# Four pairs of k tiles in w_up's second units, some weight sums made by adding DMAs, and two changes of order

## The chip, the core and the metric

The kernel runs on one core of a Trainium2 chip. The metric is the device time of one execution in microseconds (us); less is better. The core's engines work through instruction lists of their own and wait for each other by semaphores: TensorE (PE) multiplies and transposes, VectorE (DVE) and ScalarE (ACT) do elementwise work, GpSimd (POOL) and SyncE (SP) here mostly issue DMAs. A PE matmul takes its operands from SBUF and adds into a PSUM bank.

## The reference, cut to what matters

```python
u = rms_norm(x, norm_mix_w)                    # x: 256 x 2048, fp32
hq, hf, hi, hg, aq, ak, av, gates = split(u @ w_in)
y_a = rms_norm(hgrn2_scan(silu(hq), 1 - g, hi, log(g))) * silu(hg)
y_b = chunk_band_attention(aq, ak, av, rel_bias)
gate_a, gate_b = split(sigmoid(gates))
merged = gate_a * (y_a @ w_branch_a) + gate_b * (y_b @ w_branch_b)
h = x + merged @ w_out
u = rms_norm(h, norm_mlp_w)
h = h + square(relu(u @ w_up)) @ w_down        # w_up 2048 x 8192
out = rms_norm(h, norm_final_w)
```

Nearly all the time is in products of 256 rows with large fp32 weight matrices.

## The kernel before, in words

**One product.** An fp32 product is made of three matmuls (`mm3`, L145): each operand is split into a rounded high part and a low rest, and high by high, high by low and low by high are added. Weights come in raw tiles of 128 x 1024 (two k tiles by 512 columns, or one k tile by two column blocks; 512 KB) by a DMA on SP (`piece`, L673, issues at L681 and L684), and `parts` (L688) makes the high part `wh` by an ACT cast (L92) and the low part `wl` by a DVE subtraction (L93). There are eight raw buffers and six each for `wh` and `wl`; a load waits until its buffer's last reader is done, and a cast until PE is done with its buffer.

**One unit.** `gemm_s` (L720) makes 256 rows by two column blocks of 512 (n0, n1) over 16 k tiles. Of these k tiles, r pairs (k, k+4) are done together by the Strassen-Winograd scheme: seven products in place of eight. Products p1 to p7 go in the order p1, p3, p5, p2, p6, p7, p4. Their weight operands are sums of raw tiles, made in place by DVE (`adds`, L769, whose operation is L745): W22 += W12, W12 += W11, W11 += W22, W21 += W11. Their activation operands S4, S5, S2 and S7 are sums of blocks, made once per activation by `combos` (L615). What is not paired goes as plain tiles, named r0_k and r1_k for the first and second column block. With r = 4 pairs a unit has no half tiles; with r = 3 it has two tiles X and Y whose halves belong to different pairs, and their sums are of 512 columns. The names in the profile follow: `wl_dn10p` is the low part of a Strassen operand in the unit dn10, `wh_up12r` a high part of a plain tile in up12, `raw_dn` a raw tile.

**The MLP.** It runs in four quarters (qd 0 to 3) of 2048 hidden columns. A quarter has two units of w_up (up{qd}0 and up{qd}2, L1048) and two of w_down (dn{qd}0 and dn{qd}2, L1099), so that dn10 follows up12. The results of w_up are scaled, clipped and squared by ACT (`done`, L1042 and L1043), and transposed by PE into the activation u (`turn`, L1012; `tp_u`), which ACT and DVE split again; `turns` (L1028) transposes what waits, and when the first two of the four blocks of u are there, `combos` makes u's S sums for both units of w_down. The last plain tile of a unit is kept back and done within the next unit (`late`, `flush`). Results of w_down are copied by ACT and added to h by a DMA of POOL (`out_of`, L1074).

**The opening and the branches.** The kernel opens with the transposed projections hf and hq, for which PE takes pairs of k tiles as they arrive; `mm_t` (L172) makes for each k tile a matmul of 256 columns with the low weights and one of 512 with the high ones, for each of two column blocks. After the gates' projection come w_branch_a and w_branch_b: units ba0 and bb0 by `gemm_s` with r = 2 over 8 k tiles, then ba2, bb2, ba3, bb3 by `gemm2` (L705), which makes 512 columns at a time. `turn` transposes the merged blocks m0 to m3, `combos` makes their sums, and w_out's units wo0 (r = 3) and wo2 (r = 2) follow.

**What sets the order.** The functions write the instructions in one sequence; a list scheduler with priorities then orders each engine's list. Splits, weight sums and evictions carry a high priority (`tc.high_priority`). An engine executes its list strictly in order.

Of the kernel before, what the change touches and what calls it, by code (L numbers as in the profile page):

```python
# [12 lines left out]
ALU = mybir.AluOpType  # L13
# [3 lines left out]
P = 128  # L17
T = 256
NM = T // P
D = 2048  # L20
KD = D // P
# [29 lines left out]
def tile_hybrid_block(  # L51
# [120 lines left out]
    def mm_t(acc, rhs, nkt, kt, wh, wl):  # L172
        r = rhs[kt // 4][:, kt % 4]
        for cb in range(2):
            c = slice(cb * P, (cb + 1) * P)
            if kt:
                nc.tensor.matmul(acc[:, cb, 0:T], wl[:, c], r[:, 0, :], start=False, stop=False)  # L177
            nc.tensor.matmul(acc[:, cb, :], wh[:, c], r.rearrange("p u t -> p (u t)"),  # L178
                             start=kt == 0, stop=kt == nkt - 1)
            if kt == 0:  # L180
                nc.tensor.matmul(acc[:, cb, 0:T], wl[:, c], r[:, 0, :], start=False, stop=False)

    def add_parts(dst, acc):
        with tc.high_priority(offset=2000):
            nc.scalar.copy(dst, acc[:, :, T:])
            nc.vector.tensor_tensor(dst, acc[:, :, 0:T], dst, op=ALU.add)  # L186
# [17 lines left out]
        nc.sync.dma_start(xr, x[m * P:(m + 1) * P, :])  # L204
        nc.scalar.activation(xr, xr, AF.Square, accum_out=xsq[:, m:m + 1])

    done = [0, 0]
    for kt, n in zip(starts, steps):
        c, a = kt // 4, kt % 4
        xw = h2(f"xw{kt}")[:, :n]  # L210
        nc.sync.dma_start(xw, x_t[:, kt:kt + n, :])
        with tc.high_priority(offset=2000):
            for j in range(n):
                g, hi = wmix[:, kt + j:kt + j + 1], xT[c][:, a + j, 0, :]
                if kt < 2:
                    nc.vector.tensor_scalar(hi, xw[:, j, :], g, None, op0=ALU.mult)
                else:
                    nc.scalar.activation(hi, xw[:, j, :], AF.Copy, scale=g)
                nc.vector.scalar_tensor_tensor(xT[c][:, a + j, 1, :], xw[:, j, :], g, hi.bitcast(F32),
                                               op0=ALU.mult, op1=ALU.subtract)  # L220
        for i in range(2):
            while done[i] < kt + n:
                mm_t(accs[i], xT, KD, *next(ws[i]))
                done[i] += 1
    def rows(factors, what):

        wide = hp.tile([P, NM, P], F32, name=f"wide_{what}", tag="wide", bufs=1)
# [489 lines left out]
        with tc.high_priority(offset=2000):  # L717
            nc.vector.tensor_tensor(dst, acc, dst, op=ALU.add)

    def gemm_s(lhs, S, w, n0, what, done, r=R, kt0=0, between=None, front=None, fresh=False, tail=False, nkt=KD, room=None):  # L720

# [45 lines left out]
        def adds(As, Bs):  # L769
            for a, b in zip(As, Bs):  # L770
                add(a[0], b[0])
# [72 lines left out]
        if r == 3:  # L844
            mm("21", comb(7), px, (1, 2))
        u2 = copy(space(f"u2_{what}"), "21")
        adds(W21, W11)
        short = tail or len(left) == 2
        early = left[1][1] // 4 < len(lhs) and not short
        if early:  # L850
# [64 lines left out]
    def turn(n):  # L915
        mT.append(new_act(f"m{n}"))
        hi, lo = mT[n][:, :, 0, :], mT[n][:, :, 1, :]
        for m in range(NM):
            tp = transpose4(ga[n][m], f"m{n}{m}")
            split(hi[:, :, m * P:(m + 1) * P], lo[:, :, m * P:(m + 1) * P], tp)  # L920
# [27 lines left out]

    gemm_s(ya, Sy[0], w_branch_a, 0, "ba0", done_a, r=2, nkt=8, room=more[0])
    gemm_s(yb, Sy[1], w_branch_b, 0, "bb0", done_b, r=2, nkt=8, room=more[1])  # L950
    for n in range(2, 4):
        for y, w, gate, what in ((ya, w_branch_a, ga[n], "ba"), (yb, w_branch_b, gb[n], "bb")):
            acc = gemm2(y, w, n * NC, 8, f"{what}{n}", {2: flush, 6: lambda: turn(0)} if what == "ba" and n == 2 else {})
            for m in range(NM):
                gated(gate, m, acc[m])
            if (what, n) in (("bb", 2), ("ba", 3)):
                turn(len(mT))
                if n == 2:
                    Sm = combos(mT, "m", "b")
        for m in range(NM):  # L960
            both(n, m)

# [44 lines left out]
    for qd in range(NQ):  # L1007
        last = qd == NQ - 1
        uT = []
        pend = []  # L1010

        def turn(ahead=0):  # L1012

            c, rs = pend.pop(0)
            uT.append(new_act(f"u{qd}{c}"))
            hi, lo = uT[-1][:, :, 0, :], uT[-1][:, :, 1, :]
            for m in range(NM):
                tp = transpose4(rs[m], f"u{qd}{c}{m}")
                if c < 2:
                    blocks[m, c] = tk.tile([P, 4, P], F32, name=f"a{m}{c}_u{qd}", tag="t", bufs=TOK)  # L1020
                    nc.scalar.copy(blocks[m, c], tp)
                with tc.high_priority(offset=ahead):
                    split(hi[:, :, m * P:(m + 1) * P], lo[:, :, m * P:(m + 1) * P], tp)

        Su = {}
        blocks = {}

        def turns():  # L1028
            if len(hT) == 2:
                h_blocks(2)  # L1030
            while pend:
                turn()
            if len(uT) == 2:
                Su.update(combos(uT, f"u{qd}", "b", [blocks[m, j] for m in range(NM) for j in range(2)], 4))

        for c in range(0, 4, 2):
            rs = {}

            def done(m, n, acc, c=c, rs=rs):
                t = token(f"r{qd}{c}")  # L1040
                with tc.high_priority(offset=2000):
                    nc.scalar.activation(t, acc, AF.Relu, scale=rstd2[:, m:m + 1])  # L1042
                nc.scalar.activation(t, t, AF.Square)  # L1043
                rs[m, n] = t
                if m == NM - 1:
                    pend.append((c + n, [rs[i, n] for i in range(NM)]))

            gemm_s(hT, Sh, w_up, qd * (FF // NQ) + c * NC, f"up{qd}{c}", done, r=R if c else 4 if qd else 2, between=turns)  # L1048
            if not qd and not c:
                for i, s in combos(hT, "h4", None, ks=slice(R, 4), into=[Sh4[:, i:i + 1] for i in range(4)]).items():  # L1050
                    Sh[i] += s

        if last:
            wf = apool.tile([P, D], F32, name="wf", tag="act")
            nc.gpsimd.dma_start(wf, bass.AP(tensor=norm_final_w.tensor, offset=norm_final_w.offset, ap=[[0, P], [1, D]]))

        def weigh(m, n):

            t = h1[n][m]
            total = ssq3[:, m, n:n + 1] if n < 3 else rest3[:, m:m + 1]  # L1060
            nc.scalar.activation(token(f"ysq_{n}_{m}"), t, AF.Square, scale=D ** -0.5, accum_out=total)
            if n == 3:
                h1[n][m] = token(f"yw_{m}")
            nc.vector.tensor_tensor(h1[n][m], t, wf[:, n * NC:(n + 1) * NC], op=ALU.mult)

        def out_of(m, n, acc, last=last):
            r = h1[n][m]
            if last and n > 1:
                evict(r, acc)
            else:  # L1070
                t = token(f"y{qd}{n}{m}")
                with tc.high_priority(offset=2000):
                    nc.scalar.copy(t, acc)  # L1073
                nc.gpsimd.dma_start(r, t, accum_op=ALU.add)  # L1074
            if not last or n < 2:
                return
            if n == 2 and not m:
                for i in range(2):
                    for j in range(NM):
                        weigh(j, i)  # L1080
            weigh(m, n)
            if n < 3:
                if m:
                    nc.vector.tensor_reduce(most3, ssq3, axis=AX.X, op=ALU.add)
                return
            f = rstd3[:, m:m + 1]
            nc.vector.tensor_tensor(rest3[:, m:m + 1], rest3[:, m:m + 1], most3[:, m:m + 1], op=ALU.add)
            nc.gpsimd.tensor_tensor(f, rest3[:, m:m + 1], mhalf[:, 0:1], op=ALU.pow)
            for i, a, b, eng in ((0, 0, NC, nc.scalar), (2, 0, NC, nc.vector), (3, 0, NC, nc.vector),
                                 (1, 0, T, nc.scalar), (1, T, NC, nc.vector)):  # L1090
                t = h1[i][m][:, a:b]
                if eng is nc.scalar:
                    nc.scalar.activation(t, t, AF.Copy, scale=f)
                else:
                    nc.vector.tensor_scalar(t, t, f, None, op0=ALU.mult)
                (nc.scalar if eng is nc.scalar else nc.sync).dma_start(out[m * P:(m + 1) * P, i * NC + a:i * NC + b], t)

        for n0 in (0, 2):
            gemm_s(uT, Su, w_down, n0 * NC, f"dn{qd}{n0}", lambda m, n, acc, n0=n0: out_of(m, n0 + n, acc), r=4, kt0=qd * KD,  # L1099
                   front=None if n0 else lambda: turn(2000), between=None if n0 else turns, tail=last and n0 == 2)  # L1100


# [42 lines left out]
```

## Time and profile before

| what | value |
|---|---|
| median of 3 runs | 1401.89 us (1401.4 to 1402.52) |
| the profiled execution, its own time | 1402.0 us |
| span of that execution in the trace | 1400.0 us |
| mean granted TensorE clock | 0.998 |
| adding of weight sums by DVE in w_down (64) and w_up (44 full ones) | 77.3 and 53.4 us |
| loads over the span | 280 MB, 200 GB/s |

A line of the waits reads: engine and instruction that waited, the one it waited for, microseconds in total, times, longest. A line of a timeline reads: start in the span, duration, engine, line, operation, output <- inputs, shapes, count of like instructions in a row, and in brackets the engine's idle time before it and what ended it. Matmuls overlap: one of 512 columns lasts 0.39 us, but the next starts earlier. A line of the windows gives for each stretch its length and the busy time of PE, weight loads, DVE, ACT and POOL with the number of instructions, then the clock, the share of the DMA engines and GB/s. A group's line gives count, busy time, mean ns of one, and the idle time before them; a DMA's line count, KB each and the median time from issue to landing.

### The profile page before, as it was taken

The numbers are of one execution on the slowest core, as the hardware profiler recorded it, in microseconds if no ns is written. First come the engines' busy times: TensorE is split into PE (matmuls) and PEld (weight loads), VectorE is DVE, ScalarE is ACT, GpSimd is POOL, SyncE is SP. The second block draws the span as 40 slices with busy tenths as digits, with TensorE's granted clock in tenths as the row PEclk, the third lists the DMA queues.
The fourth block names the chain that finished last, engine by engine and source line by source line (L and its number), as shares of the span: only waits on it lengthen the run. The fifth ranks groups of instructions, "written<-read, shape, count | busy, mean of one in ns | idle before, by whom it ended". The sixth has DMA issues, their size and how long they took to land.

```text
span 1400.0 us, 18532 instructions
## 1 busy us (share of the span) xinstructions
PE 1386.8 (99%) x6578; PEld 1153.0 (82%) x6578; DVE 1200.9 (86%) x1558; ACT 913.2 (65%) x1236; POOL 58.0 (4%) x121
## 2 busy tenths in 40 slices
PE   9999999999999999999999999999999999999997
PEld 8889888878788888888888888888888888888886
DVE  7798987575768899988998989989989899898996
ACT  6767835464656676545666776667666776668764
POOL 2000001010100000000000001000000000000000
PEclk9999999999999999999999999999999999999999
DMA  9654545555456655756653577765678646787463
GB/s 336 221 173 144 177 146 163 193 174 169 156 181 224 212 183 206 254 182 225 212 191 131 188 241 233 212 218 161 214 255 247 202 134 231 238 272 240 137 209 120
DMA packets 115996, 280.16 MB, mean 200 GB/s; under 512 B 9792, under 2 KB 20544, under 8 KB 115520
## 3 DMA queue, kind: packets, MB, share of 16 engines
q1 hardware_dynamic: 109568, 265.59, 56.5%
q0 software_dynamic: 5616, 12.59, 4.4%
q8 instruction: 51, 0.84, 0.2%
q10 hardware_dynamic: 720, 0.81, 0.2%
q14 instruction: 41, 0.34, 0.1%
HBM read 269.51 MB, written 2.10 MB: 194 GB/s over the span
## 4 chain that ended last, share of the span: by engine, by line
PE 90%; DVE 5%; issue 1%; DMA 1%; ACT 1%; POOL 0%; SPq 0%; POOLq 0%; DVEq 0%; ACTq 0%
PE acc_ak L178 2%; PE acc_aq L178 2%; PE acc_hf L178 2%; PE acc_hq L178 1%; PE ps L391 1%; PE acc_hg L146 1%; PE acc_hg L148 1%; PE acc_hg L147 1%; PE acc_av L148 1%; PE acc_av L146 1%; PE acc_av L147 1%; PE acc_aq L177 1%; PE acc_wo2c L148 1%; PE acc_up00c L148 1%; PE acc_up00c L146 1%
## 5 line engine op out<-in xcount | busy, mean ns | idle before, releaser
L745 DVE TENSOR_TENSOR raw_dn<-raw_dn,raw_dn 128x1024 f32<-128x1024 f32 x64 | 77.3, 1218 | 0.4
L745 DVE TENSOR_TENSOR raw_up<-raw_up,raw_up 128x1024 f32<-128x1024 f32 x44 | 53.4, 1219 | 0.5
L1074 POOL DMA_DIRECT2D h<-y x28 | 23.9, 854 | 590.2 <-ACT y L1073 589.0
L178 PE MATMUL acc_aq<-act_x,wh_aq 128*128 128x512 f32 x128 | 46.5, 401 | 0.0
L178 PE MATMUL acc_hq<-act_x,wh_hq 128*128 128x512 f32 x128 | 45.8, 396 | 0.5 <-ACT wh_hq L92 0.5
L178 PE MATMUL acc_hf<-act_x,wh_hf 128*128 128x512 f32 x128 | 46.0, 397 | 0.0
L178 PE MATMUL acc_ak<-act_x,wh_ak 128*128 128x512 f32 x128 | 44.8, 396 | 0.0
L93 DVE TENSOR_TENSOR wl_av<-raw_av,wh_av 128x1024 fp32r<-128x1024 f32 x16 | 19.6, 1224 | 18.1 <-ACT wh_av L92 18.1
L177 PE MATMUL acc_hf<-act_x,wl_hf 128*128 128x256 f32 x120 | 34.2, 285 | 0.8 <-DVE wl_hf L93 0.8
L177 PE MATMUL acc_aq<-act_x,wl_aq 128*128 128x256 f32 x120 | 34.6, 288 | 0.0
L177 PE MATMUL acc_hq<-act_x,wl_hq 128*128 128x256 f32 x120 | 34.0, 283 | 0.0
L177 PE MATMUL acc_ak<-act_x,wl_ak 128*128 128x256 f32 x120 | 33.5, 279 | 0.0
L93 DVE TENSOR_TENSOR wl_aq<-raw_aq,wh_aq 128x1024 fp32r<-128x1024 f32 x16 | 19.6, 1225 | 14.3 <-ACT wh_aq L92 14.2
L92 ACT CAST wh_aq<-raw_aq 128x1024 fp32r<-128x1024 f32 x16 | 16.8, 1047 | 22.2 <-PE acc_hg L148 10.9
L93 DVE TENSOR_TENSOR wl_ga<-raw_ga,wh_ga 128x1024 fp32r<-128x1024 f32 x16 | 19.5, 1223 | 13.7 <-ACT wh_ga L92 13.5
L92 ACT CAST wh_av<-raw_av 128x1024 fp32r<-128x1024 f32 x16 | 16.8, 1053 | 22.0 <-PE acc_av L148 12.4
L92 ACT CAST wh_hg<-raw_hg 128x1024 fp32r<-128x1024 f32 x16 | 16.7, 1044 | 20.7 <-PE acc_hg L148 9.7
L178 PEld LDWEIGHTS acc_hq<-act_x,wh_hq 128*128 128x128 f32 x128 | 24.0, 188 | 6.0 <-ACT wh_hq L92 0.8
L178 PEld LDWEIGHTS acc_aq<-act_x,wh_aq 128*128 128x128 f32 x128 | 24.1, 188 | 5.6 <-issue 0.7
L178 PEld LDWEIGHTS acc_hf<-act_x,wh_hf 128*128 128x128 f32 x128 | 24.2, 189 | 5.5 <-DVE f L186 0.3
L178 PEld LDWEIGHTS acc_ak<-act_x,wh_ak 128*128 128x128 f32 x128 | 23.9, 188 | 5.4
L92 ACT CAST wh_ak<-raw_ak 128x1024 fp32r<-128x1024 f32 x16 | 16.8, 1051 | 16.7 <-PE acc_aq L178 9.1
(1300 smaller groups left out, 5167.5 us busy)
## 6 DMA issues: line engine op xcount, KB each, us to landing
raw_dn<-in_w_down_dram SPq DMA_DIRECT2D x64, 512.0 KB, 6.1
raw_up<-in_w_up_dram SPq DMA_DIRECT2D x44, 512.0 KB, 6.5
raw_ga<-in_w_in_t_dram SPq DMA_DIRECT2D x20, 512.0 KB, 3.7
raw_hi<-in_w_in_n_dram SPq DMA_DIRECT2D x16, 512.0 KB, 4.0
raw_hg<-in_w_in_n_dram SPq DMA_DIRECT2D x16, 512.0 KB, 3.7
raw_aq<-in_w_in_t_dram SPq DMA_DIRECT2D x16, 512.0 KB, 4.0
raw_ak<-in_w_in_t_dram SPq DMA_DIRECT2D x16, 512.0 KB, 3.7
raw_av<-in_w_in_n_dram SPq DMA_DIRECT2D x16, 512.0 KB, 3.9
```

The source lines that it names most:

```text
L92: (copy or nc.scalar.copy)(hi, src)
L93: nc.vector.tensor_tensor(lo, src, hi.bitcast(F32), op=ALU.subtract)
L146: nc.tensor.matmul(acc, hi, wh, start=first, stop=False, skip_group_check=True)
L147: nc.tensor.matmul(acc, hi, wl, start=False, stop=False, skip_group_check=True)
L148: nc.tensor.matmul(acc, lo, wh, start=False, stop=last, skip_group_check=True)
L177: nc.tensor.matmul(acc[:, cb, 0:T], wl[:, c], r[:, 0, :], start=False, stop=False)
L178: nc.tensor.matmul(acc[:, cb, :], wh[:, c], r.rearrange("p u t -> p (u t)"), start=kt == 0, stop=kt == nkt - 1)
L391: nc.tensor.matmul(ps[:, m, :], klf[:, a * P:(a + 1) * P], qrf[:, a * 192:(a + 1) * 192], start=True, stop=True)
L745: nc.vector.tensor_tensor(dst, dst, t, op=ALU.add)
L1074: nc.gpsimd.dma_start(r, t, accum_op=ALU.add)
```

## The change

It has four parts.

- Opening: `mm_t_high_first` takes both k tiles of a pair at once and makes the four matmuls with high weights first and then the four with low ones. The last pair goes as before.
- Branches: the transposes of m1 and the sums go from behind bb2 into its middle (at its k tile 4), the transpose of m2 from behind ba3 into its middle.
- Weight sums: with `by_dma` the sum W21 += W11 (two tiles) is made by two DMAs of POOL that add, in place of two DVE additions. It is used in up12, up22, up32, dn10, dn20 and dn30.
- w_up's second units of quarters 1 to 3 (up12, up22, up32) take r = 4 in place of 3. The second unit of quarter 0 keeps 3.

```diff
+    def mm_t_high_first(acc, rhs, items):
+
+        for low in range(2):
+            for kt, wh, wl in items:
+                r = rhs[kt // 4][:, kt % 4]
+                for cb in range(2):
+                    c = slice(cb * P, (cb + 1) * P)
+                    if low:
+                        nc.tensor.matmul(acc[:, cb, 0:T], wl[:, c], r[:, 0, :], start=False, stop=False)
+                    else:
+                        nc.tensor.matmul(acc[:, cb, :], wh[:, c], r.rearrange("p u t -> p (u t)"), start=kt == 0, stop=False)
...
         for i in range(2):
-            while done[i] < kt + n:
-                mm_t(accs[i], xT, KD, *next(ws[i]))
-                done[i] += 1
+            items = [next(ws[i]) for _ in range(n)]
+            if kt + n < KD:
+                mm_t_high_first(accs[i], xT, items)
+            else:
+                for item in items:
+                    mm_t(accs[i], xT, KD, *item)
...
         u2 = copy(space(f"u2_{what}"), "21")
-        adds(W21, W11)
+        if by_dma:
+            for a, b in zip(W21, W11):
+                nc.gpsimd.dma_start(a[0], b[0], accum_op=ALU.add)
+        else:
+            adds(W21, W11)
...
+    Sm = {}
+
+    def turn_and_sums():
+        turn(1)
+        Sm.update(combos(mT, "m", "b"))
+
+    on_the_way = {"ba2": {2: flush, 6: lambda: turn(0)}, "bb2": {4: turn_and_sums}, "ba3": {4: lambda: turn(2)}, "bb3": {}}
...
-            acc = gemm2(y, w, n * NC, 8, f"{what}{n}", {2: flush, 6: lambda: turn(0)} if what == "ba" and n == 2 else {})
+            acc = gemm2(y, w, n * NC, 8, f"{what}{n}", on_the_way[f"{what}{n}"])
             for m in range(NM):
                 gated(gate, m, acc[m])
-            if (what, n) in (("bb", 2), ("ba", 3)):
-                turn(len(mT))
-                if n == 2:
-                    Sm = combos(mT, "m", "b")
...
-            gemm_s(hT, Sh, w_up, qd * (FF // NQ) + c * NC, f"up{qd}{c}", done, r=R if c else 4 if qd else 2, between=turns)
+            gemm_s(hT, Sh, w_up, qd * (FF // NQ) + c * NC, f"up{qd}{c}", done, r=4 if qd else R if c else 2, between=turns, by_dma=qd and c)
...
-            gemm_s(uT, Su, w_down, n0 * NC, f"dn{qd}{n0}", lambda m, n, acc, n0=n0: out_of(m, n0 + n, acc), r=4, kt0=qd * KD,
+            gemm_s(uT, Su, w_down, n0 * NC, f"dn{qd}{n0}", lambda m, n, acc, n0=n0: out_of(m, n0 + n, acc), r=4, kt0=qd * KD, by_dma=qd and not n0,
```

More of the change, by code (lines that the diff above doesn't have):

```diff
@@ L205, in squares @@
         nc.scalar.activation(xr, xr, AF.Square, accum_out=xsq[:, m:m + 1])
-    done = [0, 0]
     for kt, n in zip(starts, steps):
@@ L718, in evict, with gemm_s @@
             nc.vector.tensor_tensor(dst, acc, dst, op=ALU.add)
-    def gemm_s(lhs, S, w, n0, what, done, r=R, kt0=0, between=None, front=None, fresh=False, tail=False, nkt=KD, room=None):
+    def gemm_s(lhs, S, w, n0, what, done, r=R, kt0=0, between=None, front=None, fresh=False, tail=False, nkt=KD, room=None, by_dma=False):
         n1 = n0 + NC
```

## The prediction

> **What bounds the kernel now.** I read the page's first part, then the list of PE's waits, then the windows of the three quarters that the change touches.
>
> ```profile
> PE 1386.8 (99%) x6578; PEld 1153.0 (82%) x6578; DVE 1200.9 (86%) x1558; ACT 913.2 (65%) x1236; POOL 58.0 (4%) x121
> ```
>
> ```profile
> PE ps_warm L84 <- DVE warm L82: 1.1, 1, 1.1
> PE acc_hf L177 <- DVE wl_hf L93: 0.8, 1, 0.8
> ...
> PE acc_wo0c L146 <- ACT u_wo L775: 0.5, 1, 0.5
> ```
>
> ```profile
> 968.00:1010.00 42.00, 42.00 (x196) 34.92 (x195) 38.80 (x38) 28.67 (x36) 0.51 (x1) 1.00 0.60 201
> 1136.00:1178.00 42.00, 42.00 (x195) 34.93 (x194) 38.71 (x38) 28.67 (x35) 0.85 (x1) 1.00 0.58 201
> 1303.00:1345.00 42.00, 42.00 (x195) 34.91 (x194) 38.76 (x38) 28.74 (x35) 0.35 (x1) 1.00 0.60 201
> ```
>
> PE bounds it: busy for 99% of the span, and its waits are single ones, the longest 1.1 us; of the seven in the list two lie where the change works, wl_hf and u_wo. Time goes in two ways: fewer matmuls, or those few waits. Time comes in one way: a new wait of PE. The windows (length, PE, PEld, DVE, ACT, POOL, clock, DMA share) hold dn10, dn20 and dn30. PE has no hole there and the clock is full, but DVE is busy for 38.7 to 38.8 of 42 us: what is moved ahead of a split that PE needs soon can make PE late.
>
> **The change part by part: matmuls.** A unit with three pairs has 61 products of k tiles, three matmuls each (183); with four pairs it has 60 (180). So nine matmuls go.
>
> ```profile
> 969.89 0.39 PE L146 MATMUL acc_dn10c<-wh_dn10p,act_u 128*128 128x512 f32 x1
> ...
> 972.61 1.03 PE L109 MATMUL tp_u<-ident,r 128*128 128x128 f32 x8
> 973.40 0.48 PE L146 MATMUL acc_up12c<-wh_up12r,act_h 128*128 128x512 f32 x1
> ```
>
> From 969.89 to 972.61 stand the twelve matmuls of dn10's p1: 0.227 us each. Nine are **-2.0 us**, and since PE is dense there, nothing hides them. The eight transposes take 0.79 (972.61 to 973.40).
>
> **The opening.** Its first fifteen microseconds, PE, DVE and ACT:
>
> ```profile
> 9.74 0.39 PE L178 MATMUL acc_hq<-act_x,wh_hq 128*128 128x512 f32 x1
> 10.88 0.39 PE L177 MATMUL acc_hf<-act_x,wl_hf 128*128 128x256 f32 x1 [0.76 <-DVE wl_hf L93]
> ...
> 30.92 0.50 PE L178 MATMUL acc_hf<-act_x,wh_hf 128*128 128x512 f32 x1
> ```
>
> ```profile
> 9.49 0.62 ACT L92 CAST wh_hf<-raw_hf 128x512 fp32r<-128x512 f32 x1 [0.34 <-DMA raw_hf<-in_w_in_t_dram]
> ```
>
> ```profile
> 10.14 0.69 DVE L93 TENSOR_TENSOR wl_hf<-raw_hf,wh_hf 128x512 fp32r<-128x512 f32 x1 [0.40 <-ACT wh_hf L92]
> ```
>
> The second pair begins with a low matmul, which waits until 10.83 for DVE. With the high ones first it needs only the cast, over at 10.11, and the four high matmuls (0.9 us) cover DVE's 0.7: about -0.7. From 10.88 to 30.92 are 14 groups of four high and four low, 1.43 us each; at the matmul's own 0.227 and half of that for the low ones a group is 1.36. If the regular order takes back a third of that in the 12 groups that change, -0.3; between 0 and -0.8. I take **-1.0** for the opening (-0.7 to -1.5).
>
> **The branches and w_out.** Transposes of the second and third merged block and the sums go from behind a unit into its middle. Their work is the same; the gain is in wo0, where DVE's list gets shorter:
>
> ```profile
> 639.61 1.22 DVE L745 TENSOR_TENSOR raw_wo<-raw_wo,raw_wo 128x1024 f32<-128x1024 f32 x1
> 640.86 0.80 SPq L684 DMA_DIRECT2D raw_wo0r<-in_w_out_dram  x2
> 647.01 1.05 ACT L92 CAST wh_wo0r<-raw_wo0r 128x1024 fp32r<-128x1024 f32 x1 [3.73 <-DMA raw_wo0r<-in_w_out_dram]
> 647.96 0.58 ACT L775 COPY u_wo<-acc_wo0c 128x512 f32<-128x512 f32 x1
> ```
>
> ```profile
> 647.67 0.39 PE L148 MATMUL acc_wo0c<-wh_wo0r,act_m 128*128 128x512 f32 x1
> 648.59 0.50 PE L146 MATMUL acc_wo0c<-wh_wo0p,act_m 128*128 128x512 f32 x1 [0.54 <-ACT u_wo L775]
> ```
>
> The add at 639.61 frees the buffer of the load issued at 640.86. The load lands late, its cast waits 3.73, the copy of u2 waits behind that cast, and PE behind the copy: a step of 0.92 where 0.23 is normal. In the changed program the add stands four DVE operations earlier, so the load comes some 3 us earlier and this wait goes: **-0.7**. What is late next would be the transposes inside the units, since the blocks that they read are made shortly before: between 0 and one such wait again (+0.7), I take 0.
>
> **The weight sums by DMA.** In up{q}2 and dn{q}0 (q 1 to 3) two DVE adds each go to POOL's queue: 12 DMAs of 512 KB.
>
> ```profile
> L745 DVE TENSOR_TENSOR raw_dn<-raw_dn,raw_dn 128x1024 f32<-128x1024 f32 x64 | 77.3, 1218 | 0.4
> L1074 POOL DMA_DIRECT2D h<-y x28 | 23.9, 854 | 590.2 <-ACT y L1073 589.0
> h<-y POOLq DMA_DIRECT2D x28, 256.0 KB, 3.5
> raw_dn<-in_w_down_dram SPq DMA_DIRECT2D x64, 512.0 KB, 6.1
> ```
>
> ```profile
> 985.96 1.06 ACT L92 CAST wh_dn10p<-raw_dn 128x1024 fp32r<-128x1024 f32 x1 [0.16 <-PE acc_dn10c L148]
> ```
>
> ```profile
> 976.16 4.62 DVE L93 TENSOR_TENSOR wl_dn10p<-raw_dn,wh_dn10p 128x1024 fp32r<-128x1024 f32 x4
> 980.70 1.21 DVE L745 TENSOR_TENSOR raw_dn<-raw_dn,raw_dn 128x1024 f32<-128x1024 f32 x1
> ```
>
> ```profile
> 981.99 0.33 SPq L681 DMA_DIRECT2D raw_dn10r<-in_w_down_dram  x1
> ```
>
> DVE gets 2.4 us back in each unit. In up{q}2 the larger unit eats it: one and a half more full splits there. In dn{q}0 it comes from 980.70 on, behind the place where DVE is late (below), and so moves no end. No row shows an adding DMA of 512 KB within SBUF: the 256 KB one (3.5) is the lower bound, twice that the upper; I take 5 alone and 9 for the second, nearest to the plain load's 6.1. The four splits from 976.16 are p5's second, p2's two and p6's first, so a sum may start when p2 is split (978.4 and 979.6) and is wanted by p4's first cast at 985.96, the second two casts later. With landings 5 and 9 us after the issue the sums are there at about 984 and 988: hidden, **0**. Between p2 and p4 PE still has p6, r1_8, p7 and r1_10, twelve matmuls each (2.72, four times: 10.9 us), so a late sum costs nothing at first. The wait also moves a load: the buffer that the sum reads was free when the add of 980.70 had ended, and the load of 981.99 went straight out on SP; now it goes after the landing, 2 us later, and the other loads on SP behind it. In POOL's queue only the results' adds stand behind, and PE waits for none of them.
>
> The Trainium skill (SBUF — State Buffer, "SBUF: two separate sides") warns that a DMA issued by GpSimd has its descriptors written there, and that certain DVE operations lock GpSimd out meanwhile. By that rule these 12 DMAs could come late beside a DVE that is 92% busy. The trace speaks against it: L1074's issues take 854 ns in the mean, among the same DVE operations.
>
> **The order in dn10, dn20 and dn30.** This is the dear part. Before, the sums for S4, S5, S2 and S7 of u and their splits stand ahead of the weights:
>
> ```profile
> 961.47 0.55 DVE L93 TENSOR_TENSOR S_u<-a_u,S_u 128x384 fp32r<-128x384 f32 x1
> ...
> 963.28 1.21 DVE L93 TENSOR_TENSOR wl_dn10p<-raw_dn,wh_dn10p 128x1024 fp32r<-128x1024 f32 x1
> 964.42 0.28 DVE L93 TENSOR_TENSOR S2m_u<-a_u,S2m_u 128x128 fp32r<-128x128 f32 x1
> ...
> 974.96 1.28 DVE L93 TENSOR_TENSOR act_u<-tp_u,act_u 128x512 fp32r<-128x512 f32 x2
> ```
>
> ```profile
> 978.12 0.70 ACT L1042 ACTIVATE r<-acc_up12c,rstd 128x512 f32<-128x512 f32 x1
> 978.85 0.64 ACT L1043 ACTIVATE r<-r 128x512 f32<-128x512 f32 x1
> ```
>
> so that PE goes p1, p3 (with S4), rest of up12, p5, p2. In the changed program S4's sum comes after p2's weights are split, and PE goes p1, transposes, all of the rest of up12, then p2, and only then p3. p2 is wanted six microseconds earlier, and DVE has hardly less to do before it. The walk, in before's times with PE 0.7 early (p1 at 969.2): the cast of p3's weights waits for a buffer that PE frees three pairs before p1, at 961.1; its DVE split starts at 962.45. Until p2's split come ten operations of 1.14 (964.42 less 963.28), a sum of 0.6 and two activation splits of 0.6: start 975.65, ready 976.9. PE: p1 and the rest of up12 2.72 each, transposes 0.79, one matmul of p2: 975.7, then 0.4 of transposes (they wait for ACT's square, too, about as long), so it wants the split at 976.1 and goes on at 977.3: +1.2. p2's second weights have an add ahead of them and end 0.6 later than PE wants them. S4's sum then ends at 980.3, its cast stands behind two others on ACT, 981.4, PE wants it at 980.6: +0.8. S4's low part and the add before r1_8: +0.3. That is 2.9 in dn10. dn20 and dn30 have nearly the same order and load; in dn30 the cast of p2's second weights is ahead of S4's (2.5). Sum **+8.3**, bounds 0 (every estimate 1.2 too late) and 14 (each wait counted twice, with loads moved behind it).
>
> **Sum.** The profiled execution is 1402.0 (1400.0 of span and 2.0 around), 0.1 above the median. 1402.0 - 2.0 - 1.0 - 0.7 + 8.3 - 0.1 = 1406.5.
>
> **The rivals.** *DVE is in time.* If p2's split and S4's cast come 1.2 us or more before my walk has them, PE never waits; they would if the split of p3 began at 961.2 in place of 962.45. For it: no DVE wait at all shows in these windows before. Against it: the gate is a buffer that PE frees. All 8.3 go: 1398.2, faster.
>
> *Half of it.* If the matmuls between take up the S4 terms and only p2 is late (1.3 each): 3.9 in place of 8.3: 1402.1, no change.
>
> *The DMA sums are late.* If one lands more than 8 us after its issue, p4's cast, and beyond 15 us PE itself, waits; everything behind that cast on ACT waits with it, in six units. At 3 more of landing (12 in place of 9), 1 to 2 us a unit on top: 1406.5 + 9 = 1415. For it: the DMA engines are at 60% already. Against it: 3.5 for half the bytes. This is also how the change would fail at what it says, since a sum off DVE would then cost more than on it.
>
> **How the numbers follow.** Forecast (1403.5 to 1410 by itself) 0.5; half of it 0.2; DVE in time 0.22; DMA late 0.08. A measurement here tells about 0.2% (2.8 us) from no change. Slower (above 1404.7): 0.46 of the forecast's 0.5 and the late DMAs' 0.08, together 0.54. Faster (below 1399.1): DVE in time, 0.22, and 0.02 of the half case, where the opening gives its most, 0.24. The same: 0.18 of the half case and 0.04 of the forecast, 0.22. The range from 1397.5 to 1411 holds all but the late DMAs and the far ends.
>
> **What would show it.** In the list of PE's waits: acc_dn10c, acc_dn20c and acc_dn30c on wl of p2 (DVE L93) and on S_u (ACT or DVE), 1 to 2 us each; none on raw or wh of p4; no wait any more on wl_hf and u_wo. Three windows of 42 us with PE below 40 would bear out the last term; full ones would make the time 1398, and a wait of p4 on a sum would make it over 1410.

## The result, and the profile after

The changed kernel takes 1421.18 us (1420.54 to 1423.78) against 1402.2: a ratio of 1.014, 95% interval 1.0128 to 1.0152. The forecast, slower by 4.3 us, had the sign; the size is 19.0 us, outside the range.

The list of PE's waits of the changed kernel, above 0.3 us in the quarters (waited <- waited for: total, times, longest; `by_dma` and the new functions have moved the line numbers, L1064 is the square that was L1043):

```profile
PE tp_u L109 <- DVE act_u L93: 9.0, 3, 4.6
PE acc_dn20c L146 <- ACT S_u L92: 1.5, 1, 1.5
PE tp_u L109 <- ACT r L1064: 1.2, 2, 0.6
...
PE acc_dn30c L146 <- ACT wh_dn30p L92: 1.0, 1, 1.0
...
PE acc_dn10c L147 <- DVE wl_dn10p L93: 0.4, 2, 0.3
```

Below the first line stand the waits that were forecast, in other sizes: p2's weights, S_u, the transposes behind ACT's square. The first line, 9.0 us in three waits, was not forecast. The DMAs that add, which were counted at nothing, land about as fast as was estimated:

```profile
raw_up<-raw_up POOLq DMA_DIRECT2D x6, 512.0 KB, 6.2
raw_dn<-raw_dn POOLq DMA_DIRECT2D x6, 512.0 KB, 5.1
```

No wait of PE is on the weights of a p4 (ACT waited 1.2 us once for a landing, in dn20, without a wait of PE behind it). To see in which unit the time went, I took the start of each unit's first matmul in both profiled executions and compared the distances to the next unit's (dn10 starts at 969.89 before and at 972.46 after, and so on). Differences to the kernel before, in us; the rows from e1 on are experiments described below. Each row is one profiled execution:

| kernel | up12 | up22 | up32 | sum | dn10 | dn20 | dn30 | sum |
|---|---|---|---|---|---|---|---|---|
| forecast | -0.7 | -0.7 | -0.7 | -2.0 | 2.9 | 2.9 | 2.5 | 8.3 |
| changed | 3.6 | 1.6 | 6.5 | 11.7 | 2.0 | 2.9 | 2.5 | 7.4 |
| e1 no DMA sums | 4.7 | 3.3 | 3.2 | 11.2 | 8.1 | 5.4 | 3.5 | 16.9 |
| e2 DMA sums in w_down only | 3.8 | 6.4 | 4.0 | 14.3 | 2.0 | 2.8 | 2.5 | 7.3 |
| e3 DMA sums in w_up only | 2.6 | 1.6 | 6.2 | 10.4 | 7.6 | 4.0 | 3.4 | 15.0 |
| e4 sums of u first | 1.8 | 3.1 | 5.1 | 10.0 | 1.0 | 1.5 | 1.1 | 3.6 |
| e5 transposes earlier | 0.5 | 0.3 | 3.3 | 4.0 | 0.1 | 0.1 | 0.0 | 0.2 |
| e6 the same, DMA sums in w_down only | -0.5 | -0.5 | -0.5 | -1.5 | 0.7 | 1.0 | 1.1 | 2.8 |
| e9 e6 with sums of u first | -0.5 | -0.5 | -0.5 | -1.5 | 0.1 | 0.1 | 0.0 | 0.2 |

Elsewhere in the changed kernel: opening -1.6, bb0 +1.0, wo0 -0.8, the rest (mostly the projection av and unit bb2) +0.4. That makes 18.1 at PE's end; the span grew by 18.8 (1400.0 to 1418.8), the rest of it behind PE's last instruction. So the w_down units are near the forecast, and 13.7 of the 14.7 us by which the forecast was short are in up12, up22 and up32. What happens there is on ACT. In the timeline of the kernel before, the copies of the first transposes (a_u, L1021) are over before the first weights of w_down are cast:

```profile
946.60 0.59 ACT L1021 COPY a_u<-tp_u 128x512 f32<-128x512 f32 x1
...
954.25 0.58 ACT L1021 COPY a_u<-tp_u 128x512 f32<-128x512 f32 x1
...
956.66 1.05 ACT L92 CAST wh_dn10p<-raw_dn 128x1024 fp32r<-128x1024 f32 x1
```

In the changed kernel, ACT, then PE, in the same place (PE made the first eight transposes at 952.72):

```profile
951.67 1.05 ACT L92 CAST wh_up12r<-raw_up12r 128x1024 fp32r<-128x1024 f32 x1 [0.23 <-DMA raw_up12r<-in_w_up_dram]
955.46 1.04 ACT L92 CAST wh_dn10p<-raw_dn 128x1024 fp32r<-128x1024 f32 x1 [2.73 <-DMA raw_dn<-in_w_down_dram]
956.41 0.58 ACT L1042 COPY a_u<-tp_u 128x512 f32<-128x512 f32 x1
956.88 0.59 ACT L92 CAST act_u<-tp_u 128x512 fp32r<-128x512 f32 x1
```

```profile
952.72 1.04 PE L109 MATMUL tp_u<-ident,r 128*128 128x128 f32 x8
...
958.41 0.66 PE L109 MATMUL tp_u<-ident,r 128*128 128x128 f32 x4 [2.38 <-DVE act_u L93]
```

The cast of dn10's first weights stands first in ACT's list, and its load has not landed. The weights are not wanted by PE before 972.46, 16 us later. But ACT stands still for 2.73 us, the copies and casts of the finished transposes queue behind, DVE's split behind those, and PE can't put the next transposes into the same PSUM buffers. The load comes in a burst. SP's queue and the windows (last two columns: DMA share and GB/s):

```profile
938.77 3.23 SPq L695 DMA_DIRECT2D raw_up12r<-in_w_up_dram  x2
942.10 0.41 SPq L695 DMA_DIRECT2D raw_dn<-in_w_down_dram  x1
942.60 3.08 SPq L695 DMA_DIRECT2D raw_up12r<-in_w_up_dram  x4
945.73 8.92 SPq L695 DMA_DIRECT2D raw_dn<-in_w_down_dram  x6
```

```profile
950.00:954.00 4.00, 4.00 (x23) 3.44 (x22) 3.81 (x4) 2.27 (x3) 0.00 (x0) 1.00 1.05 417
954.00:958.00 4.00, 2.04 (x9) 1.33 (x8) 1.76 (x3) 2.54 (x5) 0.00 (x0) 1.00 1.03 421
```

Thirteen loads go out within 16 us, and the DMA engines are full at about 420 GB/s: 512 KB every 1.25 us. The cast is no later than in the kernel before, though (955.46 against 956.66). What is new is its place: ahead of the copies, and not behind them.

Waiting is not all that the stall costs. The longest, in up32, and the matmuls behind it, with the window of 2 us (after the five busy columns stands the clock):

```profile
1305.84 1.12 PE L109 MATMUL tp_u<-ident,r 128*128 128x128 f32 x4 [4.61 <-DVE act_u L93]
...
1309.32 0.63 PE L148 MATMUL acc_up32c<-wh_up32r,act_h 128*128 128x512 f32 x1
1309.75 0.63 PE L146 MATMUL acc_up32c<-wh_up32r,act_h 128*128 128x512 f32 x1
...
1311.27 0.39 PE L147 MATMUL acc_up32c<-wl_up32r,act_h 128*128 128x512 f32 x1
1311.50 0.39 PE L148 MATMUL acc_up32c<-wh_up32r,act_h 128*128 128x512 f32 x1
```

```profile
1307.00:1309.00 2.00, 2.00 (x8) 1.62 (x8) 0.69 (x1) 1.36 (x3) 0.00 (x0) 0.50 0.01 4
```

The matmuls start 0.43 us apart in place of 0.23, at a granted clock of 0.50, until 1311. From the end of the wait at 1305.84 to the first fast one at 1311.03 are 5.2 us for eight transposes and eight matmuls that take 0.79 and 1.81 in the dense stretches: 2.6 lost on top of 4.6. In up12 it is 1.9 on top of 2.4 (from 958.41 to 962.92, the same work); in up22, after a wait of 2.0, the clock stays whole. Together 9.0 and 4.5 are 13.5; less the matmuls saved (1.5 in e9), 12.0: near the 11.7 of the table.

### The profile page after: what moved, and what is told of

It is laid out like the page before. It is cut to its first block, busy times and chain, and to the rows that moved or that the text cites. A ratio compares the mean times of both kernels' runs of the same rounds, so it can differ in the third digit from the quotient of the medians.

```text
span 1418.8 us, 18519 instructions
## 1 busy us (share of the span) xinstructions
PE 1392.9 (98%) x6569; PEld 1153.8 (81%) x6569; DVE 1198.6 (84%) x1549; ACT 918.3 (65%) x1239; POOL 69.3 (5%) x133
## 4 chain that ended last, share of the span: by engine, by line
PE 50%; DVE 4%; DMA 3%; issue 2%; ACT 1%; POOLq 0%; POOL 0%; DVEq 0%; ACTq 0%
DMA raw_dn<-in_w_down_dram 2%; DVE raw_dn L759 1%; PE acc_wo2c L146 1%; PE acc_up00c L146 1%; PE acc_up00c L147 1%; PE acc_wo2c L147 1%; PE acc_wo2c L148 1%; PE acc_up00c L148 1%; PE acc_up02c L148 1%; PE acc_up02c L146 1%; PE acc_wo0c L146 1%; PE acc_wo0c L148 1%; PE acc_up02c L147 1%; PE acc_wo0c L147 1%; PE acc_dn00c L148 1%
## 5 line engine op out<-in xcount | busy, mean ns | idle before, releaser
L759 DVE TENSOR_TENSOR raw_dn<-raw_dn,raw_dn 128x1024 f32<-128x1024 f32 x58 | 70.0, 1218 | 0.3
L759 DVE TENSOR_TENSOR raw_up<-raw_up,raw_up 128x1024 f32<-128x1024 f32 x50 | 60.5, 1219 | 0.4
L178 PE MATMUL acc_hq<-act_x,wh_hq 128*128 128x512 f32 x100 | 35.5, 395 | 0.0
L178 PE MATMUL acc_hf<-act_x,wh_hf 128*128 128x512 f32 x100 | 35.4, 394 | 0.0
L93 DVE TENSOR_TENSOR wl_av<-raw_av,wh_av 128x1024 fp32r<-128x1024 f32 x16 | 19.6, 1224 | 18.1 <-ACT wh_av L92 18.1
L109 PE MATMUL tp_u<-ident,r 128*128 128x128 f32 x128 | 19.8, 289 | 10.2 <-DVE act_u L93 9.0
L109 PEld LDWEIGHTS tp_u<-ident,r 128*128 128x128 f32 x128 | 15.5, 146 | 15.7 <-DVE act_u L93 10.7
L93 DVE TENSOR_TENSOR wl_ak<-raw_ak,wh_ak 128x1024 fp32r<-128x1024 f32 x16 | 19.6, 1222 | 9.6 <-ACT wh_ak L92 9.6
L177 PE MATMUL acc_hq<-act_x,wl_hq 128*128 128x256 f32 x94 | 26.7, 284 | 0.0
```

The source lines that it names most:

```text
L93: nc.vector.tensor_tensor(lo, src, hi.bitcast(F32), op=ALU.subtract)
L109: nc.tensor.transpose(tp[:, j, :], src[:, j * P:(j + 1) * P], ident)
L759: nc.vector.tensor_tensor(dst, dst, t, op=ALU.add)
```

## The experiments

e1 to e4 ran on one chip, e5 to e8 on another and e9 to e12 on a third, each group beside the kernel before (1401.91, 1401.77 and 1402.0). Times of different groups are compared through these.

**e1: no adding DMAs.**

```diff
-            gemm_s(hT, ..., r=4 if qd else R if c else 2, between=turns, by_dma=qd and c)
+            gemm_s(hT, ..., r=4 if qd else R if c else 2, between=turns)
...
-            gemm_s(uT, ..., r=4, kt0=qd * KD, by_dma=qd and not n0, ...
+            gemm_s(uT, ..., r=4, kt0=qd * KD, ...
```

> The changed kernel with all weight sums back on DVE; four pairs, opening and branches stay. Compared by stages (first matmul of a unit to that of the next), the changed kernel lost 3.6, 1.6 and 6.5 us in up12, up22 and up32 and 2.0, 2.9 and 2.5 in dn10, dn20 and dn30. Theory A: in up12, up22 and up32 the loads of the plain tiles wait until the adding DMAs have landed (SP's list stands from 934 to 941 us), the first weights of w_down come late, their cast stands on ACT ahead of the copies of the transposes, and PE waits for those. Then without the DMAs these three units give back 0.7 us each against before, and the time is about 1407 (1405 to 1410). Theory B: the order that four pairs bring (cast ahead of the copies) is enough by itself: PE still waits over 1.5 us in each of the three units, and the time is 1414 or more.

1428.78 us, ratio 1.0186 (1.0171 to 1.0201): slower than the change. My first theory had taken the late loads for the work of the sums' landings, since SP issues a load just after each (the sums of up12 land at 938.72 and 941.58, and the two loads of the row of 938.77 go out at 938.77 and 941.63). It falls: without the adding DMAs the up units lose 11.2 us, and ACT stands in the same place even longer.

```profile
950.88 1.06 ACT L92 CAST wh_up12r<-raw_up12r 128x1024 fp32r<-128x1024 f32 x1 [0.30 <-PE acc_up12c L148]
955.89 1.04 ACT L92 CAST wh_dn10p<-raw_dn 128x1024 fp32r<-128x1024 f32 x1 [3.95 <-DMA raw_dn<-in_w_down_dram]
956.84 0.58 ACT L1042 COPY a_u<-tp_u 128x512 f32<-128x512 f32 x1
```

**e2 and e3: adding DMAs in w_down only, in w_up only** (one of the two edits of e1 each).

> The changed kernel with adding DMAs in dn10, dn20 and dn30 alone. Theory A: as without any, 1405 to 1410, and the waits of tp_u on act_u (9.0 us in three times) are gone. Theory B: 1419 to 1422.

> The changed kernel with adding DMAs in up12, up22 and up32 alone. Theory A: the stalls of the up units stay whole, 1419 to 1423; if the DMAs in w_down are part of the cost, 2 us or more less than that. Theory B: 1419 to 1423 as well, with the same stalls without the DMAs of the other unit.

1421.84 (ratio 1.014, 1.0124 to 1.0155) and 1428.17 (1.0186, 1.017 to 1.0201). e2 came out as theory B said; e3 lies above what either theory gave it. The DMAs in w_up change nothing that the up units' spread lets one see, and theory B holds for the stalls. The DMAs in w_down save some 7 us, and all of it in dn10, dn20 and dn30 (16.9 and 15.0 without, 7.4 and 7.3 with them). I had put that at nothing, because the additions come behind the place where DVE is late; they do, but DVE is still late there, and without the DMAs all that follows in the unit is pushed on. A part of the 7 us is the clock: in dn10 of e1 and e3 it stood at 0.50 for 6.83 us, in dn20 of e1 for another 3.41, and in the changed kernel's w_down units never. Half of PE's busy time in these stretches is lost by it: about 3 us of dn10's loss in either run.

**e4: the sums of u with the priority of the weight splits.**

```diff
             if len(uT) == 2:
-                Su.update(combos(uT, f"u{qd}", "b", [blocks[m, j] for m in range(NM) for j in range(2)], 4))
+                with tc.high_priority(offset=2000):
+                    Su.update(combos(uT, f"u{qd}", "b", [blocks[m, j] for m in range(NM) for j in range(2)], 4))
```

> The changed kernel with the priority of weight splits for the sums of u and their splits too, so that S4's cast stands on ACT ahead of the rest of up12, and p3 comes before p2 again. Theory C (my prediction's): dn10, dn20 and dn30 lose their time because p2's split and S4 come late on DVE and ACT; then these three units fall from 7.4 us over before to under 2.5, and the time is 1414 to 1417. Rival D: they lose it because their loads come late behind the stall in the up units; then they stay at 6 or more, and the time is 1420 or more.

1419.43 (1.0136, 1.0113 to 1.0159). In the profile the w_down units fall from 7.4 to 3.6 over before, but dn12, dn22 and dn32 lose 2.0 that they had not lost, so only a quarter of it is really gone. S4's place is part of the cause (theory C), and D, with 6 or more, does not hold for these three units; yet under 2.5 and 1417 at most were expected, and the medians differ by 1.8 us only, which the two intervals do not tell apart. The up units kept 10.0.

**e5: the transposes ahead of p4.** One call is moved; p4's work then stands behind the transposes, and so do the plain tiles.

```diff
+        if between and what in ("up12", "up22", "up32"):
+            between()
+            between = None
         short = tail or len(left) == 2
         early = left[1][1] // 4 < len(lhs) and not short
```

> The changed kernel with the transposes of u0 and u1 in up12, up22 and up32 moved ahead of p4 (their inputs are long there), so that ACT's copies and casts of them stand ahead of the cast of w_down's first weights, and S4 comes early again. Taking the DMAs away (e1) did not take the stalls of the up units away, so theory A has fallen. Theory E: the loads come in a burst at the DMA engines' full rate in either case, the last of twelve some 15 us after the first; the stall is only that the transposes' copies stand on ACT behind a cast whose load is late in that burst, and the clock that falls after it. Then the three up units come to 0.7 us under before each, the w_down units to within 1 us of before, and the time is 1399 to 1404. Rival F: the burst itself is the bound; then PE waits for the weights of w_down's p1 or for the plain tiles in place of the transposes, and the time stays above 1412.

1405.4 (1.0033, 1.0016 to 1.0049): 16 us of the 19 are gone with one call moved. The w_down units are back at before's time (within 0.1; S4 comes early again, as in before), up12 and up22 lose 0.5 and 0.3; up32 still loses 3.3, and the whole is a little over the expected 1399 to 1404. Theory E stands against F: the burst of loads is the same, and PE waits for no weight. So the stall hangs on where the copies stand in ACT's list.

**e6: e5 with adding DMAs in w_down only.**

> As the run before, with the adding DMAs in w_down's units alone. Theory E: within 1.5 us of the run before, since the sums in the up units are off the path either way. If the adding DMAs in w_up relieve DVE where it is late, it is 2 us or more slower.

1403.08 (1.0008, 0.9998 to 1.0018), 2.3 under e5, and not within the 1.5 that theory E gave it. The transposes' copies, first and last, and the cast of w_down's first weights:

```profile
949.25 0.59 ACT L1045 COPY a_u<-tp_u 128x512 f32<-128x512 f32 x1
...
953.33 0.60 ACT L1045 COPY a_u<-tp_u 128x512 f32<-128x512 f32 x1
...
956.40 1.05 ACT L92 CAST wh_dn10p<-raw_dn 128x1024 fp32r<-128x1024 f32 x1 [0.94 <-DMA raw_dn<-in_w_down_dram]
```

That is before's order, and the cast may wait for its load at no cost. Here no transpose waits, in e5 three do (3.5 us): so in this order the adding DMAs of w_up do cost something. In e5's up32 the copies stood behind a cast of up32's own plain tile, whose load came at 1285.9:

```profile
1286.02 1.05 ACT L92 CAST wh_up32r<-raw_up32r 128x1024 fp32r<-128x1024 f32 x1 [1.84 <-DMA raw_up32r<-in_w_up_dram]
1286.98 0.57 ACT L1045 COPY a_u<-tp_u 128x512 f32<-128x512 f32 x1
```

That this load was held up by the sums' landings I take from the order in SP's queue of that one profile; it was not tested further. What e6 still loses in the w_down units are splits of S5:

```profile
PE acc_dn30c L148 <- DVE S5m_u L93: 0.7, 1, 0.7
...
PE acc_dn20c L148 <- DVE S5m_u L93: 0.6, 1, 0.6
...
PE acc_dn10c L148 <- DVE S5m_u L93: 0.4, 1, 0.4
```

**e7: three pairs, with the adding DMAs** (`r=R if c else 4 if qd else 2` as in before, the rest as changed).

> The changed kernel with three pairs in place of four, the adding DMAs kept. The order on ACT is then nearly that of before, copies ahead of the cast. Theory E: no wait on the transposes; the opening's gain stays: 1399 to 1402. If the adding DMAs themselves hold SP's loads enough to make PE late, 1406 or more.

1401.62 (0.9998, 0.9988 to 1.0007). The stall is all but gone: two waits of the transposes on act_u, 0.5 us together, and up22 is 0.9 longer than before. The twelve DMAs are not free even so: e8, the next run, is this kernel without them and takes 0.9 us less on the same chip. It is four pairs, by the order that they bring on ACT, that cost 19 us.

**e8 and e12: the kernel before with opening and branches new, and with the opening alone.**

> The kernel before with the new opening and the moved transposes and sums in the branches; nothing changed in the MLP. My terms: -1.0 for the opening and -0.7 for wo0's wait, 1400.2. In the changed kernel the opening gave 1.6 and wo0 0.8, and a wait in bb0 of 1.0 took some of it back: 1400.5 to 1401.5 by that.

> The kernel before with the new opening alone. e8 gave 1.0 with the branches' order as well: its stages showed 1.2 from the opening, 0.8 from wo0, and 1.0 lost in bb0 to a wait for a copy behind a cast whose load was late. If that wait comes of the moved transposes, this run keeps the opening's whole gain and lacks wo0's: 1400.5 to 1401; if the wait comes because PE is earlier than the load, it stands here too: 1401.5 to 1402.

1400.74 (0.9991, 0.9982 to 1.0) and 1401.92 (0.9998, 0.9989 to 1.0007). In e12 the opening gives 1.8 by the first unit after it, and bb0 takes 1.5 and wo0 0.5 back. ACT and the waits of PE in e12:

```profile
572.91 1.05 ACT L92 CAST wh_ba<-raw_ba 128x1024 fp32r<-128x1024 f32 x1 [2.15 <-DMA raw_ba<-in_w_branch_a_dram]
...
574.81 0.58 ACT L789 COPY more_yb<-acc_bb0c 128x512 f32<-128x512 f32 x1
```

```profile
PE acc_bb0c L146 <- ACT more_yb L789: 1.2, 1, 1.2
...
PE acc_wo0c L146 <- ACT u_wo L789: 1.0, 1, 1.0
```

It is the same thing again: a copy that PE needs stands behind a cast for a later unit whose load is late. So bb0's wait does not come from the moved transposes. It comes with the earlier opening, but not always: of the thirteen profiles with the new opening, e1's alone shows nothing lost in bb0. The load that this cast waits for took 4.5 us in e1, 4.4 in the kernel before and 6.3 in e12, where it was issued 1.8 us earlier than before and landed no earlier; why it takes so long there is open. The branches' order is what takes wo0's wait away (-0.8 in every run that has it).

**e9, e10, e11: e6 with e4's priority; the same without adding DMAs; with them in all w_down units of quarters 1 to 3.**

> Four pairs, adding DMAs in dn10, dn20 and dn30 alone, the transposes ahead of p4 and the sums of u with the priority of the weight splits: both orders mended. In e6 the three w_down units still lost 0.7 to 1.1 us each to S5m's split on DVE, and e4 showed that this priority takes most of such waits away. Theory C with E: 1399.5 to 1401.5, that is up to 2 us less than before; all that the nine matmuls and the opening give, less the wait in bb0. Rival: DVE is full there and each split put ahead makes another late: 1402.5 or more.

> The same without any adding DMA, all weight sums on DVE. In the changed kernel the DMAs of the three w_down units saved some 8 us (e1 against e2), because DVE was late there. If DVE is late there only through the order, this run is within 1 us of e9; if it is full, 3 us or more slower.

> As e9, with adding DMAs in dn12, dn22 and dn32 too. PE waits for nothing in those units in any profile, so within 1 us of e9; more if a landing holds loads there as it did in up32 of e5.

1400.4 (0.9989, 0.998 to 0.9998), 1401.18 (0.9993, 0.9985 to 1.0002) and 1407.72 (1.0033, 1.002 to 1.0045). e9 beats both kernels, by 1.6 us (its interval ends just below 1) and by about 21. Its longest waits of PE are all outside the MLP:

```profile
PE ps_warm L84 <- DVE warm L82: 1.1, 1, 1.1
PE ps L405 <- DVE sd L422: 0.7, 1, 0.7
PE acc_bb0c L146 <- ACT more_yb L789: 0.6, 1, 0.6
```

e10 says that the DMAs are worth at most about a microsecond once the order is right (the intervals of e9 and e10 overlap): DVE was late through the order. e11 refutes what I expected: in dn12, dn22 and dn32 the profile shows a wait of 0.9 each on the copy u_dn that stands behind ACT's other work, and 1.2 lost a unit. That is 3.7 of the 7.3 us over e9; the execution in the profile took 1404.81, and what its slower ones lost beyond that no trace shows.

## Why the prediction was wrong

- **The matmuls, -2.0: the step that failed.** It said that nine matmuls go "and since PE is dense there, nothing hides them". In up12, up22 and up32 of the changed kernel PE is not dense: it loses 9.0 us waiting for transposes and 4.5 to the clock, 11.7 net in place of -2.0. I walked DVE's and ACT's lists through the w_down units only. In the up units I did not ask what stands in ACT's list behind a cast whose load may be late. The prediction has this very chain at wo0 (a late load, its cast, a copy behind the cast, PE behind the copy) and does not look for it where the change sets a cast ahead of other copies. Where the order is mended (e6, e9), the units give 0.5 each, three quarters of the term.
- **The order in dn10, dn20, dn30, +8.3: right in mechanism and sum.** 7.4, by unit 2.0, 2.9 and 2.5 for 2.9, 2.9 and 2.5, with waits at the places named; e4 and e5, which bring S4 forward, take away half of it (some of which comes back in the next unit) and all of it. That two units agree to a tenth is luck. By the steps from start to start, p2's weights and the squares together cost 1.2, 1.1 and 2.3 us and S4's terms 0.4, 1.7 and 0.3, where the walk had 1.8 and 1.1 in dn10. p2's split (`wl`) makes PE wait in dn10 alone, 0.4 us in place of 1 to 2 in each unit. Of the three windows of 42 us that were to show PE below 40, moved to where these units now lie, one does (41.6, 39.9 and 40.4).
- **The opening, -1.0.** -1.6 by the first unit, in other runs of the same opening -0.8 to -1.8; but most of the gain is given back in bb0 (1.0 here, 1.5 of 1.8 in e12), which I had not seen. **wo0, -0.7:** -0.8, by the step named.
- **The sums by DMA, 0.** The landings were estimated at 5 and 9 us and measured at 4.4 to 7.3; PE never waits for a p4. But "moves no end" was wrong in the changed order, where DVE is late in the w_down units: there the sums on DVE cost some 7 us more (e1 against e2). And the sums of w_up, counted at no cost, cost 2.3 us in one order (e5 against e6); by the one profile it is the load that goes out after the landing.
- **The rivals.** DMA late, with 1415 and the only one above the range, came nearest to the size and had not the cause. DVE in time falls. The late sums did let a wait pass on through a cast on ACT, but the wait for a sum; no rival let the wait for a load of the next unit pass to PE's transposes.
- The Trainium skill's rule on GpSimd's descriptors (SBUF — State Buffer, "SBUF: two separate sides") I had set aside by the issues' 854 ns. The adding DMAs' issues take 848 in the median, beside a DVE as busy: nothing here shows that DVE held them up.

## What to carry to other kernels

An engine's list is a queue: when a change reorders it, ask of every instruction in it that may wait for a load who stands behind it, also where the load's own data are not wanted for a long time. A cast for the next unit ahead of an eviction that PE needs now turns a harmless late load into a stall of PE. And walk every stage that the change touches, first of all the one in which the work gets less.

## What was not expected of the hardware

A stall of PE can cost half again through the clock. After the wait of 2.38 us the granted clock was 0.50 from 959.47 to 962.88, and during the wait of 4.61 us it fell too, from 1304.22 to 1311.05. It is not the length of the wait alone. In e3 a wait of 2.97 left it whole:

```profile
959.57 0.66 PE L109 MATMUL tp_u<-ident,r 128*128 128x128 f32 x4 [2.97 <-DVE act_u L93]
```

```profile
961.00:963.00 2.00, 2.00 (x11) 1.61 (x10) 1.29 (x2) 2.00 (x4) 0.00 (x0) 1.00 0.01 2
```

What decides shows when the trace is cut where the clock changes. In every kept trace the changes lie whole multiples of 3.41 us apart (341.34 from 962.88 to 1304.22 is a hundred of them). So time falls into stretches of 3.41 us, and the question is how much of one stretch PE is idle. The changed kernel, the stretch ahead of the first fall and the one behind it, then e3's two stretches that share the wait of 2.97 (length, PE's busy time first; third column from the end: clock):

```profile
956.06:959.47 3.41, 1.05 (x7) 0.82 (x8) 2.52 (x3) 2.75 (x6) 0.00 (x0) 1.00 1.03 422
959.47:962.88 3.41, 3.41 (x11) 2.78 (x10) 1.88 (x3) 2.73 (x5) 0.00 (x0) 0.50 0.04 17
```

```profile
954.90:958.31 3.41, 1.71 (x8) 1.09 (x6) 1.17 (x2) 1.70 (x3) 0.00 (x0) 1.00 1.03 420
958.31:961.73 3.42, 2.16 (x13) 1.79 (x14) 2.26 (x4) 2.76 (x6) 0.00 (x0) 1.00 0.51 207
```

PE idles 2.36 us of the one stretch, and 1.70 and 1.26 of the two. Two waits of 2.0 differ in the same way: the changed kernel's in up22 is split (0.93 and 1.06) and the clock stays whole, e5's in up32 lies in one stretch (1.93) and the clock falls. In the kept traces the clock falls fifteen times between the opening and the end; the stretch ahead held 1.87 to 3.22 us of idle time in fourteen cases and 1.65 in one, and no stretch that was followed by a full clock held more than 1.7. No run set the idle time on purpose, so a border near 1.7 to 1.9 us is read off these cases and not tested.

The Trainium skill (TensorE: Matmul & The Clock Gate, "Part 1: The HAM clock gate (the "warmup" mystery)") says that the gate halves the clock after an idle window of about 3.4 us, and that the window runs freely, so that its phase decides. The trace agrees with the halving (0.43 us a matmul), with the length of the window (3.41 us) and with a phase that the kernel does not set. It differs in one thing: the window need not be idle throughout, since 2.36 us of it were enough.
